# A macaron decoder layer on one core: first weights of output parts split ahead of the last gate, the memory's squares summed by token, the position table written by head, and row sums' tiles made in pairs

## The chip, the cores and the metric

The kernel runs on one core of a Trainium2 chip. The metric is the device time of one execution in microseconds (us), lower is better. A core has a matmul engine (PE, with its weight loads PEld), three engines for elementwise work (DVE, ACT, POOL), and SP, which here only issues DMAs. ACT and POOL issue DMAs too. Each engine works through its own instructions in order and waits for the others at semaphores.

## The reference

One layer on x (512 tokens by 1024), in float32, with a memory of 256 tokens. All but the mixer's scan and the softmaxes is matrix products:

```python
x = x + 0.5 * swiglu(rms_norm(x, w1), ffn1_w_in, ffn1_w_out)          # D_FF = 2816
x = x + hybrid_mixer(rms_norm(x, wm), ...)       # SSD heads + differential attention, out projection
x = x + memory_cross_attention(rms_norm(x, wc), rms_norm(mem, wmem), w_cq, w_ck, w_cv, w_co)
x = x + 0.5 * swiglu(rms_norm(x, w2), ffn2_w_in, ffn2_w_out)
return rms_norm(x, w_final)

def swiglu(h, w_in, w_out):
    gate, up = split(h @ w_in, 2)
    return (silu(gate) * up) @ w_out
```

`rms_norm(mem, w)` needs the sum of squares of each memory token over 1024 features. The differential attention adds a bias that depends on the distance of query and key only, one row of values for each of 8 heads.

## The kernel before, in words

**Numbers in two halves.** A float32 operand is split into a high part (fp32r, written by ACT, `split_into`, L155) and the rest (written by DVE, L156). A product is three matmuls: high by high, low by high, high by low. So every weight tile (512 KB, `wr`) that a DMA brings in becomes `wh` on ACT and then `wl` on DVE before PE can use it. There are six `wr` buffers; activations, gates, sums and the like share a pool of 128x512 slots (`s2`), handed out in turn.

**FFNs by blocks.** The two FFNs are computed with products of 2x2 blocks (Strassen's scheme). In the first FFN the inner width is taken in three thirds (`ffn1`, loop over `THIRDS`). In each, `ffn_quads` forms gate and up products (`qa`, `qb`, `qe`), multiplies them (`gated`: the gate's activation on ACT L442, the products on DVE L444), and `block_tiles` splits the result into the blocks 11, 22, 12 and the sums S1 to S4 (`g11h`, `s31h`, `s24h`, `gh` on ACT and their low parts on DVE). All but the last of these are spawned as chains with steps some us apart; the last is done at once.

Then `out_blocks` multiplies by the output weights of the third, in parts of two tiles: `product` over B11 into `oa`, over B12 + B11 (S1) into `oe`, in turn part by part, then S2 into `ob`, block 12 into `oa`, S3 into `ob`, S4 into `oe`, block 22 into `ob`. Sums of weight blocks are made on the way: `added` fetches one block by SP (L1220) and adds the other by an accumulating DMA that POOL issues (L1265); `t2` adds a third block on DVE (L1275). The fetches of the first two thirds are 512 KB; in the third third the second part has half the width.

**Order.** `Order` (`od`) interleaves one dense stream, which keeps a clock `od.t` of PE's work, with spawned chains that become due at times given in their `yield`s. That fixes the order in which the instructions are written down. SP and POOL keep this order; PE, ACT and DVE are ordered by a scheduler with its own estimates, within limits such as `behind`, which keeps an instruction after others.

**Beside the third third** `beside` spawns `prepare` and `memory_in`. `prepare` loads the bias table and one-hot rows, multiplies them (`prel`), copies the result with a scale on ACT (`hot`), writes it to memory (`rel_d`, two DMAs on ACT's queue) and then expands it with one DMA of 2.6 MB to `rel_z`, 128 copies for each of 8 heads; the attention later reads its bias from there (`ask_bias`). `memory_in` loads the transposed memory, squares each of its 8 tiles on ACT, adds them on DVE (`nacc`), splits the tiles into `hm`, and `finish` sums over partitions with matmuls into `nps`.

**Row sums.** `row_of` turns a column of 1/rms values into a row spread over partitions: for its high and low part it makes a diagonal tile (`ndiag`, L368) and multiplies it with ones (`nrow`), one after the other: diag, matmul, diag, matmul. The norms use DVE for it, the SSD groups POOL (after `yield W["gn"]`).

Of the kernel before, what the change touches and what calls it, by code (L numbers as in the profile page):

```python
# [11 lines left out]
F32 = mybir.dt.float32  # L12
# [5 lines left out]
P = 128  # L18
T = 512
# [16 lines left out]
LEAD = 4  # L36

W = {"h0": 3.4, "hs": 3.3, "hv": 2.08, "hp": 6.75}
W |= {"g0": 8.28, "gc": 0.75, "gx": 0.92, "gb": 2.59, "gs": 0.51, "gt": 2.0, "gd": 6.9, "gy": 0.38, "gq": 11.02, "gn": 6.52}
W |= {"c0": 4.97, "cs": 3.0, "ct": 4.82}  # L40

SPLIT, AHEAD = 5, 2
# [58 lines left out]
def body(tc, a, dbg=None):  # L101
# [255 lines left out]
        G.tensor_tensor(col, v, mhalf[:, :nb], ALU.pow)  # L357
        return col

    def row_of(col, nb, first, second):  # L360
        ch = tiny.tile([P, nb], R32, tag="ch", name=nm("ch"))
        V.tensor_copy(ch, col)
        cl = small("cl", nb)
        V.tensor_tensor(cl, col, ch.bitcast(F32), ALU.subtract)
        pr = aux("nrow", (P, nb * P))
        for j, (eng, c) in enumerate(((first, ch.bitcast(F32)), (second, cl))):
            diag = s2("ndiag", R32, (P, nb, P))
            eng.tensor_tensor(diag, ident[:, None, :].to_broadcast([P, nb, P]), c[:, :, None].to_broadcast([P, nb, P]), ALU.mult)  # L368
            with behind(list(newest_mm)):
                mm(pr, ones_r, diag.rearrange("p a b -> p (a b)"), j == 0, j == 1)  # L370
        return pr

    class Stat:
# [14 lines left out]
        def finish(self, apart=2.5):  # L388
# [4 lines left out]
            yield from self.from_sums(ps, apart)  # L393

        def from_sums(self, ps, apart=2.5):
            nb = self.n // P
            self.col = inv_rms_cols(ps, nb, 1.0 / D, EPS)
            yield apart
            pr = row_of(self.col, nb, V, V)
            self.row = s2("row", shape=(P, nb * P))  # L400
            S.activation(self.row, pr, AF.Copy)

# [2 lines left out]

    def normed(st, c, dst, sums):

        both = small("nboth", 4)
        V.tensor_tensor(both, sums[:, :4], sums[:, 4:], ALU.add)
        yield from st.from_sums(both)  # L410
        hf = {}
        for k in range(KT + 1):
            if k < KT:
                hf[k] = s2("hf")
                V.scalar_tensor_tensor(hf[k], x[k], par[:, c + k : c + k + 1], st.row, ALU.mult, ALU.mult)
            if k > 0:
                dst.append(split("hn", hf.pop(k - 1)))
                yield 1.6
# [9 lines left out]
        else:  # L428
            V.tensor_tensor(th[:, 0:2], halves(pu), halves(gate), ALU.mult)

    def ffn_quads(xs, wq, st, nq, made, places, sums=None, fresh=False):

        for q in range(nq):
            for out in quad(xs, next(wq), next(sums) if sums else None, fresh and q == 0):
                if out is None:
                    yield
            gs, us = out
            gate, th = s4("gate"), s4("th")
            for i in range(2):
                row = st.row[:, None, i * H : (i + 1) * H].to_broadcast([P, 2, H])  # L440
                V.tensor_tensor(gate[:, 2 * i : 2 * i + 2], halves(gs[i]), row, ALU.mult)
            S.activation(gate, gate, AF.Silu)  # L442
            for i in range(2):
                V.tensor_tensor(th[:, places[i]], halves(us[i]), gate[:, 2 * i : 2 * i + 2], ALU.mult)  # L444
            made(th)
            yield

    BY_BLOCK = slice(0, None, 3), slice(1, 3)

    def block_tiles(g, n):  # L450
# [12 lines left out]
        def made(th):  # L463
            g.append({})
            if len(g) < n:
                od.spawn(steps(th, g[-1], 2.9), 2.9)
            else:
                for _ in steps(th, g[-1], 0.0):
                    pass
        return made  # L470

    def ffn_first(h, wa):
# [9 lines left out]
    def ffn1(h, wa, at_out, each, done):  # L482
        xs = []
        wq, plain = iter(a["f1q"]), a["f1i"]

        def by_token():
            for k in range(KT):
# [3 lines left out]
        for ti, (_, nf) in enumerate(THIRDS):  # L491
            g = []
            nq = nf // 2
            made = block_tiles(g, nq)
            if ti == 0:
                th, f = s4("th"), 0
                for ps in ffn_first(h, wa):
# [3 lines left out]
                        gated(*ps, st1.row, th, f)  # L501
                        f += 1
                made(th)
                col4, ncol4 = small("col4", 4, bufs=1), small("ncol4", 4, bufs=1)
# [16 lines left out]
                h.clear()  # L521
                od.spawn(by_token(), 8.0)
                nq -= NPLAIN // 2
            yield from ffn_quads(xs, wq, st1, nq, made, BY_BLOCK)
            at_out(ti)
            yield from out_blocks(a[f"f1b{ti}"], None, g, col4, ncol4, each if ti == len(THIRDS) - 1 else None)
        done()
        banks = [acc, aux, acc, aux]
        yield from turn(1, banks)
# [13 lines left out]
    def beside(ti):  # L543
        if ti == 0:
            od.spawn(lambdas())
        elif ti == 2:
            od.spawn(prepare())
            od.spawn(memory_in(hm), 1.0)
# [15 lines left out]
        od.spawn(normed(st_mix, C_MIX, h, squares), 2.0)  # L564
        od.spawn(block_sums_in_dram(), 10.0)

    od.spawn(st1.finish(), 18.0)
    od.add(ffn1(h1, wa_s, beside, square, fin1))


# [24 lines left out]
    def prepare():  # L595
        rel_sb = small("rel_sb", 8, bufs=1)[:NUM_BUCKETS]
        nc.sync.dma_start(rel_sb, a["rel_bias"])
        hot = [s2("hot", shape=(NUM_BUCKETS, H)) for _ in range(2)]
        for i in range(2):
            nc.sync.dma_start(hot[i], a["hot"][:, i * H : (i + 1) * H])  # L600
        rel_far = small("rel_far", 64, bufs=1)[:8]
        V.memset(rel_far, MASKED)
        yield 9.0
        prel = aux("prel", (8, T))
        for i in range(2):
            mm(prel[:, i * H : (i + 1) * H], rel_sb, hot[i], True, True)
        for c in range(T, RW, 64):
            S.dma_start(rel_d[:, c : c + 64], rel_far)
        yield 1.5
        for i in range(2):  # L610
            S.activation(hot[i][:8], prel[:, i * H : (i + 1) * H], AF.Copy, scale=-8.0)
        yield 2.0
        for i in range(2):
            S.dma_start(rel_d[:, i * H : (i + 1) * H], hot[i][:8])
        yield 6.0
        S.dma_start(rel_z[:, :, :RW], rel_d[:, None, :].to_broadcast([8, P, RW]))

    def bc_c(t):
        return t[:, None, :].to_broadcast([P, 4, 16])
# [99 lines left out]
    def queries_keys(hd):  # L719
        if hd == 0:  # L720
            ask_bias(0)
        if hd < 7:
            ask_bias(hd + 1)
        pq = acc("pq")
        yield from proj(pq, load_w(a["wq"][hd]), h)
        q = split("q", pq, -1.0)
# [147 lines left out]
    def group(g, bt, ct, xs, zs):  # L874
# [99 lines left out]
        rh = small("rh", 4)  # L974
        V.tensor_scalar(rh, rr, 0.5, None, ALU.mult)
        yield W["gn"]
        pr = row_of(rh, 4, G, G)
# [10 lines left out]
    def memory_tile(k, queue=nc.sync):  # L988
        mk = s2("mem", shape=(P, MEM))
        queue.dma_start(mk, a["memT"][k])  # L990
        return mk

    def memory_in(dst):
        mem = []
        for k in range(0, KT, 2):
# [216 lines left out]
    def out_blocks(blocks, sums, g, col4, ncol4, each=None, finale=None, clean=True):  # L1212


        n = len(g)
        parts = [(k, min(k + 2, n)) for k in range(0, n, 2)]

        def fetch(of, part):
# [20 lines left out]
                    newest_mm[:] = [nc.tensor.matmul(ps, a_[:, ts], b_[:, ws], start=first and k == 0 and j == 0, stop=k == n - 1 and j == 2, skip_group_check=True).ins]  # L1239
                yield  # L1240

        def product(ps, of, which, first=False):
            for part in parts:
                w = weights(of, part)
                for t in range(2):
                    yield from some(ps[t], w, which, part, t, first)

# [3 lines left out]
            if each is not None and done:  # L1251
                each(tb, half_)

        bank = [acc, aux]
        a_ps = [bank[t]("oa") for t in range(2)]
        e_ps = [bank[t]("oe") for t in range(2)]
        b_ps = [bank[t]("ob") for t in range(2)]
        if clean:
            nc.tensor.matmul(b_ps[1], ones_r, ones_r[:, None, :].to_broadcast([P, 4, P]), start=True, stop=True)
        t_raw = {}  # L1260

        def added(of, more):
# [144 lines left out]
def layout(i):  # L1407
# [7 lines left out]
    d = {}  # L1415
    d["xT"] = np.ascontiguousarray(i["x"][0].T).reshape(KT, P, T)
    d["xt"] = np.ascontiguousarray(i["x"][0].reshape(4, P, 2, T).transpose(2, 0, 1, 3)).reshape(KT, P, T)
    d["memT"] = np.ascontiguousarray(i["mem"][0].T).reshape(KT, P, MEM)
    for n, s in (("1", "ffn1"), ("2", "ffn2")):
        wi = tiles(i[f"{s}_w_in"][0]).reshape(2 * NF, P, KT // 2, 2, P)  # L1420
# [58 lines left out]
```

## Time and profile before

| | us |
|---|---|
| median of 3 runs | 1327.48 |
| lowest and highest | 1323.78, 1330.71 |
| the profiled execution | 1326.33 |
| its span | 1324.2 |
| PE busy in it | 1295.8 |

Times in the rows of a profile are counted from the start of the span. Rows of a timeline give start, duration, engine, line, operation, output from inputs, and in brackets how long the engine stood idle before and what released it. A trailing h or l in a tile's name is the high or low part. Rows of windows give the stretch, its length, the busy time and instructions of PE, PEld, DVE, ACT and POOL, the granted clock of PE as a share, the DMA engines' share and GB/s.

### The profile page before, as it was taken

Reading aid. Unit: us, or ns where it says so; the run is one execution under the profiler, and the core shown is the slowest. Engines: PE = TensorE matmul, PEld = TensorE weight load, DVE = VectorE, ACT = ScalarE, POOL = GpSimd, SP = SyncE. Lnnn points to the kernel's source line nnn. Section 1 sums busy time; section 2 is a strip of 40 time slices with the busy share of each in tenths; the row PEclk is TensorE's granted clock in tenths of the full one; section 3 lists DMA queues with packets and bytes.
Section 4 is the critical chain, followed back from the end, with each engine's and each line's share of the span. In section 5 each row is a group of like instructions: output and inputs, shape, how many; then the busy total and the mean of one; then the engine's idle time right before and its main releaser. Section 6 shows DMA issues by size and latency. Waiting matters only on the chain.

```text
span 1324.2 us, 20141 instructions
## 1 busy us (share of the span) xinstructions
PE 1295.8 (98%) x7728; PEld 1127.3 (85%) x7728; DVE 988.1 (75%) x1570; ACT 708.4 (53%) x1192; POOL 124.8 (9%) x143
## 2 busy tenths in 40 slices
PE   9999999998989999999999999999999999999996
PEld 7898998897877778777788877888889999989995
DVE  7988789787866586557867686645678878877886
ACT  6544556455844465336644556434455645555564
POOL 0001010001110011110112021020001000000001
PEclk9999999999999999999999999999999999999998
DMA  7567767874794533763465547684238876656662
GB/s 272 163 171 211 179 176 198 216 204 122 241 351 133 154 66 97 252 176 100 92 201 180 167 128 232 196 208 142 65 96 244 227 226 185 189 193 178 186 203 87
DMA packets 69431, 235.28 MB, mean 178 GB/s; under 512 B 8072, under 2 KB 9576, under 8 KB 68984
## 3 DMA queue, kind: packets, MB, share of 16 engines
q1 hardware_dynamic: 52912, 180.19, 40.1%
q0 software_dynamic: 12880, 44.62, 19.0%
q10 hardware_dynamic: 3544, 9.20, 1.9%
q8 instruction: 60, 0.98, 0.3%
q14 instruction: 35, 0.29, 0.1%
HBM read 231.82 MB, written 50.91 MB: 214 GB/s over the span
## 4 chain that ended last, share of the span: by engine, by line
PE 86%; issue 7%; DVE 4%; DMA 1%; ACT 1%; POOL 1%; POOLq 0%; ACTq 0%; DVEq 0%
PE qb L240 12%; PE pm L146 9%; PE qe L240 8%; PE qa L240 8%; PE ob L1239 6%; PE pxbc L146 5%; PE oe L1239 4%; PE oa L1239 4%; PE pk L146 3%; PE pq L146 3%; PE pcq L146 3%; PE pv L146 3%; PE pz L146 2%; PE pa L146 2%; PE pg L146 2%
## 5 line engine op out<-in xcount | busy, mean ns | idle before, releaser
L155 ACT ACTIVATE wh<-wr 128x1024 fp32r<-128x1024 f32 (+1 forms) x329 | 334.6, 1019 | 368.8 <-issue 54.6
L156 DVE TENSOR_TENSOR wl<-wr,wh 128x1024 fp32r<-128x1024 f32 (+1 forms) x329 | 386.1, 1176 | 141.5 <-ACT wh L155 139.1
L146 PE MATMUL pxbc<-hnh,wh 128*128 128x512 f32 x128 | 52.3, 408 | 0.0
L146 PE MATMUL pxbc<-hnh,wl 128*128 128x512 f32 x128 | 50.3, 393 | 0.0
L146 PE MATMUL pxbc<-hnl,wh 128*128 128x512 f32 x128 | 50.2, 392 | 0.0
L748 ACT ACTIVATE ec<-ec,mn 128x512 f32<-128x512 f32 (+3 forms) x64 | 35.4, 555 | 24.1 <-DVE mn L747 24.1
L240 PE MATMUL qb<-s31h,wh 128*128 128x256 f32 x152 | 43.1, 284 | 0.0
L240 PE MATMUL qe<-s31h,wl 128*128 128x256 f32 x152 | 43.1, 283 | 0.0
L240 PE MATMUL qa<-h11h,wh 128*128 128x256 f32 x152 | 43.1, 283 | 0.0
L240 PE MATMUL qa<-h11h,wl 128*128 128x256 f32 x152 | 43.0, 283 | 0.0
L240 PE MATMUL qb<-s24h,wl 128*128 128x256 f32 x152 | 43.0, 283 | 0.0
L240 PE MATMUL qa<-hmh,wh 128*128 128x256 f32 x152 | 43.0, 283 | 0.0
L240 PE MATMUL qa<-hml,wh 128*128 128x256 f32 x152 | 43.0, 283 | 0.0
L240 PE MATMUL qe<-s24h,wh 128*128 128x256 f32 x152 | 43.0, 283 | 0.0
L240 PE MATMUL qe<-s24l,wh 128*128 128x256 f32 x152 | 43.0, 283 | 0.0
L240 PE MATMUL qe<-s24h,wl 128*128 128x256 f32 x152 | 43.0, 283 | 0.0
L240 PE MATMUL qb<-hmh,wh 128*128 128x256 f32 x152 | 43.0, 283 | 0.0
L240 PE MATMUL qb<-hml,wh 128*128 128x256 f32 x152 | 43.0, 283 | 0.0
L240 PE MATMUL qb<-hmh,wl 128*128 128x256 f32 x152 | 43.0, 283 | 0.0
L240 PE MATMUL qb<-s24l,wh 128*128 128x256 f32 x152 | 43.0, 283 | 0.0
L240 PE MATMUL qb<-s24h,wh 128*128 128x256 f32 x152 | 43.0, 283 | 0.0
L240 PE MATMUL qb<-s31h,wl 128*128 128x256 f32 x152 | 43.0, 283 | 0.0
(447 smaller groups left out, 4184.3 us busy)
## 6 DMA issues: line engine op xcount, KB each, us to landing
wr<-in_f2q SPq DMA_DIRECT2D x44, 512.0 KB, 4.4
wr<-in_f1q SPq DMA_DIRECT2D x40, 512.0 KB, 4.6
wr<-in_f1b SPq DMA_DIRECT2D x30, 512.0 KB, 4.9
isum<-in_f2q SPq DMA_DIRECT2D x22, 512.0 KB, 5.3
wr<-isum SPq DMA_DIRECT2D x22, 512.0 KB, 4.5
wsum<-in_f2b SPq DMA_DIRECT2D x20, 512.0 KB, 5.1
wr<-wsum SPq DMA_DIRECT2D x20, 512.0 KB, 4.6
wr<-in_f1q POOLq DMA_DIRECT2D x16, 512.0 KB, 6.4
```

The source lines that it names most:

```text
L146: newest_mm[:] = [nc.tensor.matmul(out, w, x, start=start, stop=stop).ins]
L155: S.activation(hi, src, AF.Copy),
L156: V.tensor_tensor(lo, src, hi.bitcast(F32), ALU.subtract),
L240: newest_mm[:] = [nc.tensor.matmul(out, a_[:, wc], b_, start=first and f == 0 and kp == 0 and j == 0, stop=kp == n - 1 and j == 2, skip_gr ...
L748: S.activation(ec[:, :n], ec[:, :n], AF.Exp, bias=mn, scale=-1.0, accum_out=sm[c][:, i : i + 1])
L1239: newest_mm[:] = [nc.tensor.matmul(ps, a_[:, ts], b_[:, ws], start=first and k == 0 and j == 0, stop=k == n - 1 and j == 2, skip_group_che ...
```

## The change

- `out_blocks` gets the number of its parts ahead of time and is begun inside `ffn_quads`, before the last gate of each third of the first FFN (`prime`): it fetches and splits the first part's weights of B11 and S1 there, and yields. The last `block_tiles` is placed behind these splits (`tied`).
- The memory's sums of squares come from a second layout of the memory (`memt`, by token): four tiles of 128x512, loaded on SP in the second third, squared on ACT with a sum along the row. The eight squares, the additions and the matmuls into `nps` go.
- `rel_z` is expanded by head: heads 0 and 1 by ACT's queue in `prepare`, the other six by SP's queue, one in the step of each of the heads 0 to 5.
- `row_of` makes both diagonal tiles, yields (`apart`), and does both matmuls. The planned times gq and gn change, gr is new.

```diff
+W |= {... "gq": 11.8, "gn": 5.0, "gr": 3.0}        # were gq 11.02, gn 6.52
-    def row_of(col, nb, first, second):
+    def row_of(col, nb, first, second, apart):
...
+        diags = []
+        for eng, c in ((first, ch.bitcast(F32)), (second, cl)):
+            diags.append(s2("ndiag", R32, (P, nb, P)))
+            eng.tensor_tensor(diags[-1], ident..., c..., ALU.mult)
+        yield apart
         pr = aux("nrow", (P, nb * P))
-        for j, (eng, c) in enumerate(((first, ch.bitcast(F32)), (second, cl))):
-            diag = s2("ndiag", R32, (P, nb, P))
-            eng.tensor_tensor(diag, ident..., c..., ALU.mult)
-            with behind(list(newest_mm)):
-                mm(pr, ones_r, diag..., j == 0, j == 1)
+        with behind(list(newest_mm)):
+            for j in range(2):
+                mm(pr, ones_r, diags[j]..., j == 0, j == 1)
...
     def ffn_quads(..., prime=None):
             gs, us = out
+            if prime and q == nq - 1:
+                next(prime)
             gate, th = s4("gate"), s4("th")
...
     def made(th):
-                for _ in steps(th, g[-1], 0.0):
-                    pass
+                with behind(list(recent) if tied else []):
+                    for _ in steps(th, g[-1], 0.0):
+                        pass
...
     def ffn1(h, wa, at_out, each, done):
+            out = out_blocks(a[f"f1b{ti}"], None, g, col4, ncol4, ..., n=nq)
-            yield from ffn_quads(xs, wq, st1, nq, made, BY_BLOCK)
+            yield from ffn_quads(xs, wq, st1, nq, made, BY_BLOCK, prime=out)
             at_out(ti)
-            yield from out_blocks(a[f"f1b{ti}"], None, g, col4, ncol4, ...)
+            yield from out
...
     def beside(ti):
+        elif ti == 1:
+            od.spawn(memory_squares())
...
     def prepare():
-        S.dma_start(rel_z[:, :, :RW], rel_d[:, None, :].to_broadcast([8, P, RW]))
+        for hd in range(2):
+            expand_bias(S, hd)
+
+    def expand_bias(queue, hd):
+        queue.dma_start(rel_z[hd, :, :RW], rel_d[hd : hd + 1].to_broadcast([P, RW]))
...
     def queries_keys(hd):
+        if hd < 6:
+            expand_bias(nc.sync, hd + 2)
...
+    def memory_squares():
+        mt = [s2("memt") for _ in range(4)]
+        for j in range(4):
+            nc.sync.dma_start(mt[j], a["memt"][j])
+        yield 12.0
+        for j in range(4):
+            with behind(list(recent)):
+                S.activation(mt[j], mt[j], AF.Square, accum_out=msq[:, j : j + 1])
+            yield 4.0
 
     def memory_in(dst):
...
-                st_mem.add(mk)
...
-        yield 3.0
-        yield from st_mem.finish(10.0)
+        both = small("nboth", 4, bufs=2)[:, :2]
+        V.tensor_tensor(both, msq[:, :2], msq[:, 2:], ALU.add)
+        yield from st_mem.from_sums(both, 10.0)
...
     def out_blocks(..., n=None):
+        ready = [None, None]
+        if early:
+            ready = [weights(of, parts[0]) for of in (blocks[B11], sums[0])]
+            yield
         bank = [acc, aux]
...
-        both = [product(a_ps, blocks[B11], "11", True), product(e_ps, sums[0], S1, True)]
+        both = [product(a_ps, blocks[B11], "11", True, ready[0]), product(e_ps, sums[0], S1, True, ready[1])]
```

The host lays the memory out a second time for `memt`.

More of the change, by code (lines that the diff above doesn't have):

```diff
@@ L38 @@
 W = {"h0": 3.4, "hs": 3.3, "hv": 2.08, "hp": 6.75}
-W |= {"g0": 8.28, "gc": 0.75, "gx": 0.92, "gb": 2.59, "gs": 0.51, "gt": 2.0, "gd": 6.9, "gy": 0.38, "gq": 11.02, "gn": 6.52}
+W |= {"g0": 8.28, "gc": 0.75, "gx": 0.92, "gb": 2.59, "gs": 0.51, "gt": 2.0, "gd": 6.9, "gy": 0.38, "gq": 11.8, "gn": 5.0, "gr": 3.0}
 W |= {"c0": 4.97, "cs": 3.0, "ct": 4.82}
@@ L364, in row_of @@
         V.tensor_tensor(cl, col, ch.bitcast(F32), ALU.subtract)
-        pr = aux("nrow", (P, nb * P))
-        for j, (eng, c) in enumerate(((first, ch.bitcast(F32)), (second, cl))):
-            diag = s2("ndiag", R32, (P, nb, P))
-            eng.tensor_tensor(diag, ident[:, None, :].to_broadcast([P, nb, P]), c[:, :, None].to_broadcast([P, nb, P]), ALU.mult)
-            with behind(list(newest_mm)):
-                mm(pr, ones_r, diag.rearrange("p a b -> p (a b)"), j == 0, j == 1)
+        diags = []
+        for eng, c in ((first, ch.bitcast(F32)), (second, cl)):
+            diags.append(s2("ndiag", R32, (P, nb, P)))
+            eng.tensor_tensor(diags[-1], ident[:, None, :].to_broadcast([P, nb, P]), c[:, :, None].to_broadcast([P, nb, P]), ALU.mult)
+        yield apart
+        pr = aux("nrow", (P, nb * P))
+        with behind(list(newest_mm)):
+            for j in range(2):
+                mm(pr, ones_r, diags[j].rearrange("p a b -> p (a b)"), j == 0, j == 1)
         return pr
@@ L386, in add, with finish @@
                 V.tensor_tensor(self.acc, self.acc, sq, ALU.add)
-        def finish(self, apart=2.5):
+        def finish(self, apart=2.5, rows=1.2):
             nb = self.n // P
@@ L392, in finish, with from_sums @@
                 mm(ps[:, b : b + 1], self.acc[:, b * P : (b + 1) * P], ones[:, 0:1], True, True)
-            yield from self.from_sums(ps, apart)
-        def from_sums(self, ps, apart=2.5):
+            yield from self.from_sums(ps, apart, rows)
+        def from_sums(self, ps, apart=2.5, rows=1.2):
             nb = self.n // P
@@ L398, in from_sums @@
             yield apart
-            pr = row_of(self.col, nb, V, V)
+            pr = yield from row_of(self.col, nb, V, V, rows)
             self.row = s2("row", shape=(P, nb * P))
@@ L406, in normed @@
     def normed(st, c, dst, sums):
-        both = small("nboth", 4)
+        both = small("nboth", 4, bufs=2)
         V.tensor_tensor(both, sums[:, :4], sums[:, 4:], ALU.add)
@@ L429, in gated, with ffn_quads @@
             V.tensor_tensor(th[:, 0:2], halves(pu), halves(gate), ALU.mult)
-    def ffn_quads(xs, wq, st, nq, made, places, sums=None, fresh=False):
+    def ffn_quads(xs, wq, st, nq, made, places, sums=None, fresh=False, prime=None):
         for q in range(nq):
@@ L448, in body, with block_tiles @@
     BY_BLOCK = slice(0, None, 3), slice(1, 3)
-    def block_tiles(g, n):
+    def block_tiles(g, n, tied=False):
         def steps(th, blocks, apart):
@@ L484, in ffn1 @@
         wq, plain = iter(a["f1q"]), a["f1i"]
+        col4, ncol4 = small("col4", 4, bufs=1), small("ncol4", 4, bufs=1)
         def by_token():
@@ L493, in ffn1 @@
             nq = nf // 2
-            made = block_tiles(g, nq)
+            made = block_tiles(g, nq, True)
+            out = out_blocks(a[f"f1b{ti}"], None, g, col4, ncol4, each if ti == len(THIRDS) - 1 else None, n=nq)
             if ti == 0:
@@ L503, in ffn1 @@
                 made(th)
-                col4, ncol4 = small("col4", 4, bufs=1), small("ncol4", 4, bufs=1)
                 V.tensor_scalar(col4, st1.col, 0.5, None, ALU.mult)
@@ L523, in ffn1 @@
                 nq -= NPLAIN // 2
-            yield from ffn_quads(xs, wq, st1, nq, made, BY_BLOCK)
+            yield from ffn_quads(xs, wq, st1, nq, made, BY_BLOCK, prime=out)
             at_out(ti)
-            yield from out_blocks(a[f"f1b{ti}"], None, g, col4, ncol4, each if ti == len(THIRDS) - 1 else None)
+            yield from out
         done()
@@ L565, in fin1 @@
         od.spawn(block_sums_in_dram(), 10.0)
-    od.spawn(st1.finish(), 18.0)
+    od.spawn(st1.finish(rows=0.0), 18.0)
     od.add(ffn1(h1, wa_s, beside, square, fin1))
@@ L976, in group @@
         yield W["gn"]
-        pr = row_of(rh, 4, G, G)
+        pr = yield from row_of(rh, 4, G, G, W["gr"])
         for j in range(2):
@@ L991, in memory_tile @@
         return mk
+    msq = small("msq", 4, bufs=1)
+    def memory_squares():
[7 more added lines that the diff above has]
+            yield 4.0
     def memory_in(dst):
@@ L1210, in block_sums_in_dram, with out_blocks @@
                 yield 9.0
-    def out_blocks(blocks, sums, g, col4, ncol4, each=None, finale=None, clean=True):
-        n = len(g)
+    def out_blocks(blocks, sums, g, col4, ncol4, each=None, finale=None, clean=True, n=None):
+        early = n is not None
+        n = n or len(g)
         parts = [(k, min(k + 2, n)) for k in range(0, n, 2)]
@@ L1240, in some, with product @@
                 yield
-        def product(ps, of, which, first=False):
+        def product(ps, of, which, first=False, ready=None):
             for part in parts:
-                w = weights(of, part)
+                w = ready if ready and part == parts[0] else weights(of, part)
                 for t in range(2):
@@ L1252, in update @@
                 each(tb, half_)
[L1254 to L1259, printed above, removed]
         t_raw = {}
@@ L1285, in out_blocks @@
             sums = [t1, added(blocks[B12], blocks[B22]), t2, lambda part: t_raw[part]]
-        both = [product(a_ps, blocks[B11], "11", True), product(e_ps, sums[0], S1, True)]
+        ready = [None, None]
+        if early:
+            ready = [weights(of, parts[0]) for of in (blocks[B11], sums[0])]
+            yield
+        bank = [acc, aux]
+        a_ps = [bank[t]("oa") for t in range(2)]
+        e_ps = [bank[t]("oe") for t in range(2)]
+        b_ps = [bank[t]("ob") for t in range(2)]
+        if clean:
+            nc.tensor.matmul(b_ps[1], ones_r, ones_r[:, None, :].to_broadcast([P, 4, P]), start=True, stop=True)
+        both = [product(a_ps, blocks[B11], "11", True, ready[0]), product(e_ps, sums[0], S1, True, ready[1])]
         for _ in parts:
@@ L1417, in layout @@
     d["xt"] = np.ascontiguousarray(i["x"][0].reshape(4, P, 2, T).transpose(2, 0, 1, 3)).reshape(KT, P, T)
+    d["memt"] = np.ascontiguousarray(i["mem"][0].reshape(2, P, 2, T).transpose(2, 0, 1, 3)).reshape(4, P, T)
     d["memT"] = np.ascontiguousarray(i["mem"][0].T).reshape(KT, P, MEM)
```

## The prediction

> **What bounds the kernel now.** I read the page first (busy time by engine, the chain that ended last), then the waits of PE, then the timelines of PE, ACT, DVE, POOL and SP around each of them.
>
> ```profile
> PE 1295.8 (98%) x7728; PEld 1127.3 (85%) x7728; DVE 988.1 (75%) x1570; ACT 708.4 (53%) x1192; POOL 124.8 (9%) x143
> PE 86%; issue 7%; DVE 4%; DMA 1%; ACT 1%; POOL 1%; POOLq 0%; ACTq 0%; DVEq 0%
> ```
>
> PE is busy 1295.8 of 1324.2 us. The change takes next to no matmul away, so it can only act on the 28 us that are left, on slow-clock matmuls behind long gaps, and on gaps that it makes itself. The waits of PE say where those 28 us are:
>
> ```profile
> PE oe L1239 <- ACT wh L155: 4.4, 1, 4.4
> PE pck L146 <- DVE wl L156: 3.8, 1, 3.8
> ...
> PE oe L1239 <- DVE wl L156: 1.7, 1, 1.7
> PE nrow L146 <- POOL ndiag L368: 1.1, 1, 1.1
> PE pm L146 <- DVE x L825: 0.9, 1, 0.9
> PE pn L146 <- POOL ysq L967: 0.8, 2, 0.5
> ...
> PE oe L1239 <- DVE s31l L156: 0.6, 1, 0.6
> PE nrow L146 <- DVE ndiag L368: 0.5, 1, 0.5
> ```
>
> The edits aim at four of these rows: the first weights of S1 (oe, 4.4), the cross-attention keys (pck, 3.8), and the two nrow rows. A long gap costs more than its length:
>
> ```profile
> 319.73 0.80 PE L1239 MATMUL oe<-wh,s31h 128*128 128x512 f32 x1 [4.44 <-ACT wh L155]
> 324.34 0.39 PE L1239 MATMUL oa<-wh,g11h 128*128 128x512 f32 x1
> 319.70:323.20 3.50, 3.43 (x8) 2.29 (x9) 3.49 (x5) 1.02 (x2) 0.00 (x0) 0.52 0.13 28
> 375.00:378.00 3.00, 3.00 (x17) 3.00 (x17) 3.00 (x5) 1.40 (x3) 0.00 (x0) 0.55 0.99 329
> ```
>
> Behind the 4.44 us gap the granted clock (third number from the end) is 0.52 for 3.5 us. The twelve oe matmuls take 324.34 - 319.73 = 4.61 us; at the usual spacing (below) they would take 2.73, so the slow clock costs 1.9 us. Behind the 3.8 us gap the clock is 0.55 for 3 us: 3 x 0.45 = 1.4 us.
>
> **Second third of the first FFN: the memory loads.** Here the change adds four loads of memt, put on SP's queue behind the two primed fetches and ahead of the second parts of B11 and B12. They take generic 128x512 slots. By the built order the fourth load may start only when the last gate product (th<-c,gate) has read its slot, and all later SP fetches stand behind it.
>
> ```profile
> 199.63 32.47 SPq L1220 DMA_DIRECT2D wr<-in_f1b  x10
> 212.70 0.40 PE L1239 MATMUL oa<-wh,g11h 128*128 128x512 f32 x1
> 215.82 0.68 DVE L444 TENSOR_TENSOR th<-c,gate 128x512 f32<-128x512 f32 x1
> 216.10 1.06 ACT L155 ACTIVATE wh<-wr 128x1024 fp32r<-128x1024 f32 x1 [0.92 <-DMA wr<-in_f1b]
> 217.19 1.22 DVE L156 TENSOR_TENSOR wl<-wr,wh 128x1024 fp32r<-128x1024 f32 x1 [0.70 <-ACT wh L155]
> 218.16 0.39 PE L1239 MATMUL oa<-wh,g11h 128*128 128x512 f32 x1
> 220.88 0.39 PE L1239 MATMUL oe<-wh,s31h 128*128 128x512 f32 x1
> wr<-in_f1b SPq DMA_DIRECT2D x7, 512.0 KB, 4.9
> DMA to landing us min/median/max: 6.1/7.2/8.3
> ```
>
> In these rows SP issues the out-weights from 199.63 on, long before they are needed. PE does B11 and S1 of the first part from 212.70 (24 matmuls to 218.16, 0.2275 each), B11 of the second part at 218.16 and S1 of the second part at 220.88. The last row is POOL's accumulating DMA (L1265) in 216 to 240 us, the next to last SP's fetch around here.
>
> After the change: gate product ends about 216.4 (215.82 + 0.68, perhaps a little less as DVE is freer); fourth memt issued about 216.4; B11 second part about 216.8, landed 4.9 later, 221.7; its wh 222.8 (1.06). PE wanted it at 218.16: a wait of 4.6, then wl 1.22 behind wh against two matmuls of 0.23, another 0.8, then the slow clock. But the end is set by B12: issued about 217.2, landed 222.1, accumulated on POOL 7.2, 229.3, wh 230.4. S1 of the second part starts at 230.4 in place of 220.88, 9.5 later; the first wait lies inside this. The 0.6 on s31l, which stood there, goes (with its ramp 0.7); wl (0.3) and some slow clock (0.5) come on top. **Loss 9.6.** Upper bound: the accumulate at 8.3 and the full slow clock, 9.6 + 1.1 + 1.4, with 0.6 for wl behind other DVE work: 12.7. Lower bound: SP doesn't hold, and only ACT's new order counts, in which wh of B11's second part stands behind gate, g11h, s31h, s24h and gh. From the third third:
>
> ```profile
> 312.38 0.40 PE L1239 MATMUL oa<-wh,g11h 128*128 128x512 f32 x1
> 318.12 0.61 ACT L155 ACTIVATE gh<-th 128x512 fp32r<-128x512 f32 x1
> ```
>
> gh ends 6.35 after the first oa, so here at 219.05; wh at 220.1, 2.0 late, and 0.8 for wl: loss 2.7. I take 9.6, since the slot and the queue order are both fixed in the built program and only durations are open.
>
> [...]
>
> **Third third: priming.** S1's first wh now stands ahead of the gate, so the 4.4 us wait and its 1.9 us go: oa and oe of the first part run 312.38 to 317.83.
>
> ```profile
> 329.20 1.02 PE L146 MATMUL prel<-hot,rel_sb 32*8 32x256 f32 x4
> 330.26 0.64 ACT L611 ACTIVATE hot<-prel 8x256 f32<-8x256 f32 x2 [1.33 <-PE prel L146]
> 330.66 0.63 ACTq L614 DMA_DIRECT2D rel_d<-hot  x2
> 335.08 0.74 ACTq L616 DMA_DIRECT2D rel_z<-rel_d  x1
> wr<-in_f1b SPq DMA_DIRECT2D x1, 256.0 KB, 2.6
> 327.59 1.74 POOL L1265 DMA_DIRECT2D wr<-in_f1b  x2 [19.87 <-DVE x L1250]
> wr<-in_f1b POOLq DMA_DIRECT2D x2, 512.0 KB, 5.6
> 336.40 0.39 PE L1239 MATMUL ob<-wh,s31h 128*128 128x512 f32 x1
> 342.91 0.50 PE L1239 MATMUL oe<-wl,s24h 128*128 128x512 f32 x1 [1.73 <-DVE wl L156]
> ```
>
> But the built order now puts prel right behind that oe (to 318.85), and on ACT hot, both rel_d issues and two rel_z issues, which wait for rel_d to land, ahead of wh of B11's second part. From these rows: hot from 318.9, rel_d issued by 319.9. The landing of rel_d has no row; between 0 and the 2.6 of a 256 KB load, I take 2.3, since the two DMAs are tiny and most of it is not bytes: 322.2. Then two rel_z issues (under 0.74 each, say 0.8 together) and wh (0.62 at half width, by gh's row): 323.6. PE waits 4.8 in place of 4.4, slow clock again. B11's second part then runs to 326.9, S1's to 328.2; before, S1's second part ran from 325.70 (4.44 + 1.9 behind) to 327.06, and prel (1.0), then still due, is already done: 0.2 late. B12's accumulate for S3 is issued once the sum behind the late wl is done (325.5), landed 330.3, accumulated (5.6) 335.9, wh 337.0, against 336.6 when PE wants it: 0.4. The 1.73 us wait for wl at 342.91 can shrink, as the memory's squares and their additions are gone from ACT and DVE: I take 1.0 of it. **Gain 0.4**; from 4 lost (accumulate at 8.3 and the 1.73 staying) to 3 gained (rel_d landing at once).
>
> **Table by head.**
>
> ```profile
> SPq L174 <- DMA rel_z<-rel_d: 14.5, 1, 14.5
> 369.23 1.06 ACT L155 ACTIVATE wh<-wr 128x1024 fp32r<-128x1024 f32 x1 [6.40 <-DMA wr<-in_wck]
> 374.65 0.58 PE L146 MATMUL pck<-hm,wl 128*128 128x256 f32 x1 [3.80 <-DVE wl L156]
> ```
>
> SP stands 14.5 us until the 2.6 MB rel_z has landed; the keys' weights come late, ACT waits 6.4 and PE 3.8. With two heads on ACT's queue and six singly on SP's, nothing in the built order waits for so long a transfer. What goes is 3.8 and 1.4 of slow clock. The same bytes still move beside the weights (DMA share 0.99 in 375 to 378), so I leave 0.4: **gain 4.8**, between 0 and 5.2.
>
> **Row sums in pairs.** Both ndiag tiles are made, then a yield of 1.2 (3.0 for groups), then both matmuls. That lifts the nrow waits, 1.1 and 0.5; gn falls from 6.52 to 5.0 and gq rises to 11.8, which can move pn's 0.8 and pm's 0.9 either way. **Gain 1.6**, from 1 lost (pn a tile late) to 2.5. The squares by token replace eight Squares, seven additions and two nps matmuls by four Squares and an addition; on PE that is nothing, its cover being that ACT is 53% busy.
>
> **The sum.** 9.6 - 0.4 - 4.8 - 1.6 = 2.8 us lost. Against the profiled execution's 1326.33 (span 1324.2 and 2.1 around it): 1329.1. The median of the runs shown is 1.15 higher: 1330.3, 0.2% slower. About 0.5% (6.6 us) is what a measurement of this kernel can tell from no change, so my number lies inside that.
>
> **Rivals.**
> (a) Everything dearer: POOL's accumulate at its slow end in both thirds, 12.7 and 4 lost: 1330.3 + 3.1 + 4.4 = 1337.8. For it: five queued 512 KB fetches then share the DMA engines with it. Against: 7.2 already holds some of that.
> (b) The loads don't hold SP, because the fourth slot's last reader is an earlier product than I read, and only ACT's order costs: 2.7 for 9.6, 1323.4; with rel_d landing at once, 1320.8: faster than before. It decides if B12's second part is issued before about 207.7 (220.88 less 1.06, 7.2 and 4.9). For it: SP ran 13 us ahead before (199.63 against 212.70). Against: the gate product needs the last qb, which ends at 212.7.
> (c) The pck wait stays, because the six table DMAs on SP or the DMA share replace it: 1335.1. Against: they are placed behind the keys' weights.
>
> **Chances.** Forecast 0.40, of which 0.07 ends slower by over 0.5% and 0.33 within it; (a) 0.25, slower; (b) 0.25, 0.15 faster by over 0.5% and 0.10 within; (c) 0.10, slower. Faster 0.15, same 0.43, slower 0.42. The range 1319 to 1341 takes in (b) with most of its bonus and (a) with 3 us on top.
>
> **What would show it.** Right: in the profile after, a PE wait of some 4 us on oa's wh and another ahead of oe in the second third, with SP's second-part fetches issued after 216 us; no S1 wait of 4.4 in the third third but one of 4 to 5 on oa behind rel_z's issue; no 14.5 us wait of SP on rel_z and no pck wait over 1; no nrow wait over 0.5. Wrong: second-part fetches issued before 210, PE's gap in the third third under 2, or new waits in the head stage behind the six table DMAs.

## The result: slower, 1341.14 us against 1328.5, and the profile after

The changed kernel takes 1341.14 us (median of 4 runs, 1339.67 to 1341.93); the kernel before takes 1328.5 (1323.78 to 1330.71, now in four runs). The ratio is 1.0099, interval 1.0069 to 1.0128. That is slower by about 1%, beyond the forecast of 1330.3 and just outside its range (up to 1341). The profiled execution has a span of 1339.8 us, 15.6 more than before. That is 3 us more than the medians differ by (12.6), so what the traces say of the size of a stage holds for one execution of each kernel.

The waits of PE after the change, in the same form as before (waiting engine, tile, line, what it waited for, total, times, longest):

```profile
PE oa L1266 <- ACT wh L155: 7.9, 3, 4.0
PE oe L1266 <- ACT wh L155: 7.7, 2, 5.5
PE pq L146 <- DVE vl L156: 3.7, 1, 3.7
...
PE ob L1266 <- ACT wh L155: 0.9, 1, 0.9
PE pn L146 <- POOL ysq L982: 0.8, 1, 0.8
```

The pck wait of 3.8 and both nrow waits are gone, as meant. In their place stand waits for split weights (oa, oe) of 15.6 us in all and a new one of 3.7 on values (pq for vl). Where they stand is seen by setting the same product's start in the two traces side by side:

| product | before | after | later by | change since the row above |
|---|---|---|---|---|
| second third, first oa | 212.70 | 213.16 | 0.5 | |
| third third, first oa | 312.38 | 326.58 | 14.2 | +13.7 |
| transposes pxf, behind the first FFN | 350.75 | 369.90 | 19.2 | +5.0 |
| first pq, behind the keys | 384.46 | 397.38 | 12.9 | -6.2 |
| pk behind the values and pq | 578.10 | 596.49 | 18.4 | +5.5 |
| first qe of the second FFN | 1000.70 | 1016.46 | 15.8 | -2.6 |

**Second third (+13.7).** Timelines of SP, DVE, ACT, POOL and PE of the changed kernel:

```profile
204.93 11.90 SPq L1013 DMA_DIRECT2D memt<-in_memt  x4
216.88 19.72 SPq L1247 DMA_DIRECT2D wr<-in_f1b  x8
215.79 0.68 DVE L449 TENSOR_TENSOR th<-c,gate 128x512 f32<-128x512 f32 x1
221.26 1.06 ACT L155 ACTIVATE wh<-wr 128x1024 fp32r<-128x1024 f32 x1 [1.74 <-DMA wr<-in_f1b]
223.80 0.85 POOL L1286 DMA_DIRECT2D wr<-in_f1b  x1 [23.72 <-DVE wl L156]
232.67 1.06 ACT L155 ACTIVATE wh<-wr 128x1024 fp32r<-128x1024 f32 x1 [6.35 <-DMA wr<-in_f1b]
222.37 0.80 PE L1266 MATMUL oa<-wh,g11h 128*128 128x512 f32 x1 [3.34 <-ACT wh L155]
233.78 0.79 PE L1266 MATMUL oe<-wh,s31h 128*128 128x512 f32 x1 [5.52 <-ACT wh L155]
238.91 0.40 PE L1266 MATMUL ob<-wh,s24h 128*128 128x512 f32 x1
```

SP spends 11.9 us on the four memory loads; the last is issued when th<-c,gate has ended (215.79 + 0.68), and the output weights follow from 216.88, where before they were issued from 199.63. B11's second part is split at 221.26, B12's second part is accumulated by POOL from 223.80 and split at 232.67. PE waits 3.34 and 5.52, and both times restarts slowly (matmuls of 0.63 us and a spacing of 0.43 in place of 0.2275). Three rows give the sizes: SP's output-weight fetches in 213 to 232, POOL's accumulate there, and the window of the first restart and the second wait:

```profile
wr<-in_f1b SPq DMA_DIRECT2D x7, 512.0 KB, 7.6
wr<-in_f1b POOLq DMA_DIRECT2D x1, 512.0 KB, 8.8
222.00:232.00 10.00, 5.86 (x12) 3.64 (x12) 2.45 (x2) 0.90 (x2) 0.85 (x1) 0.67 0.96 301
```

The 7.6 is a median. The fetch of B11's second part landed faster: it was issued at 216.88 and its split began at 221.26. In the kernel before, POOL's accumulate of the same tile stood here, with its time to landing:

```profile
206.87 0.85 POOL L1265 DMA_DIRECT2D wr<-in_f1b  x1 [9.95 <-DVE wl L156]
DMA to landing us min/median/max: 9.1/9.1/9.1
```

So this accumulate was no slower after the change (8.8 for 9.1); it only began 16.9 us later.

**Third third (+5.0, with the old wait of 4.4 gone).** Timelines of ACT and PE, and the waits of SP:

```profile
333.21 0.64 ACT L620 ACTIVATE hot<-prel 8x256 f32<-8x256 f32 x2 [0.26 <-PE prel L146]
333.61 0.63 ACTq L623 DMA_DIRECT2D rel_d<-hot  x2
335.27 1.22 ACTq L629 DMA_DIRECT2D rel_z<-rel_d  x2
336.53 0.63 ACT L155 ACTIVATE wh<-wr 128x512 fp32r<-128x512 f32 x1 [2.68 <-issue]
337.21 0.50 PE L1266 MATMUL oa<-wh,g11h 128*128 128x512 f32 x1 [4.04 <-ACT wh L155]
355.69 0.79 PE L1266 MATMUL oe<-wh,s24h 128*128 128x512 f32 x1 [2.17 <-ACT wh L155]
SPq L1247 <- DMA rel_d<-hot: 17.2, 1, 17.2
```

ACT issues rel_z ahead of the split of B11's second part, as forecast, and PE waits 4.04. The last row was not forecast: SP stands 17.2 us, until rel_d has landed, ahead of a fetch of output weights that has nothing to do with it. In the built program that fetch is given the same completion semaphore (the counter that tells of a DMA's landing) as the second rel_d DMA, eight DMAs earlier in the written order, and may start only when that one has landed. All later output weights come late, and PE pays again at S3 (0.9) and S4 (the wait of 2.17).

**Keys (-6.2).** PE's waits have no row for pck any more. SP's one wait for rel_z is 1.5 us in place of 14.5.

**Values (+5.5).** PE, ACT and DVE of the changed kernel, then PE and ACT of the kernel before at the same place:

```profile
583.63 0.62 PE L146 MATMUL nrow<-ndiag,ones_r 128*128 128x512 f32 x2
584.28 1.41 DVE L995 SCALAR_TENSOR_TENSOR y<-y,par,nrow 128x512 f32<-128x512 f32 x2 [2.22 <-PE nrow L146]
585.07 0.63 ACT L155 ACTIVATE ysh<-y 128x512 fp32r<-128x512 f32 x1 [4.26 <-DVE y L995]
587.20 2.04 ACT L155 ACTIVATE vh<-pv 128x512 fp32r<-128x512 f32 x4
589.30 0.50 PE L146 MATMUL pq<-hnh,wh 128*128 128x512 f32 x1 [3.66 <-DVE vl L156]
```

```profile
567.32 0.62 PE L146 MATMUL nrow<-ndiag,ones_r 128*128 128x512 f32 x2
571.05 1.55 ACT L155 ACTIVATE vh<-pv 128x512 fp32r<-128x512 f32 x3
572.58 0.45 PE L146 MATMUL pq<-hnh,wh 128*128 128x512 f32 x1
```

Before, the row of sums came 5.3 us ahead of pq; after, seven matmuls ahead of the end of the values. ACT holds the splits of y ahead of those of the values in its order; they wait for nrow, the values' splits stand behind them, and pq needs the bank that these free. The wait of 3.66 and the slow restart behind it (24 pq matmuls in 7.19 us for 5.52) take 5.3 us.

### The profile page after: what moved, and what is told of

The parts are those of the page before. It is cut to its first block, busy times and chain, and to the rows that moved or that the text cites. A ratio compares the mean times of both kernels' runs of the same rounds, so it can differ in the third digit from the quotient of the medians.

```text
span 1339.8 us, 20126 instructions
## 1 busy us (share of the span) xinstructions
PE 1303.0 (97%) x7724; PEld 1131.8 (84%) x7724; DVE 985.9 (74%) x1564; ACT 709.6 (53%) x1192; POOL 124.0 (9%) x143
## 3 DMA queue, kind: packets, MB, share of 16 engines
q0 software_dynamic: 12880, 44.62, 19.2%
## 4 chain that ended last, share of the span: by engine, by line
PE 91%; DMA 3%; DVE 3%; ACT 2%; issue 1%; POOL 0%; ACTq 0%; SPq 0%; POOLq 0%; DVEq 0%
PE qb L240 12%; PE pm L146 9%; PE qe L240 8%; PE qa L240 8%; PE pxbc L146 7%; PE ob L1266 6%; PE oe L1266 4%; PE oa L1266 4%; PE pq L146 3%; PE pk L146 3%; PE pcq L146 3%; PE pz L146 3%; PE pv L146 3%; PE pck L146 2%; PE pcv L146 2%; PE pg L146 2%
## 5 line engine op out<-in xcount | busy, mean ns | idle before, releaser
L240 PE MATMUL qa<-hmh,wl 128*128 128x256 f32 x152 | 43.0, 283 | 0.0
L240 PE MATMUL qa<-h11l,wh 128*128 128x256 f32 x152 | 43.0, 283 | 0.0
```

The costliest lines, as they stand in the source:

```text
L240: newest_mm[:] = [nc.tensor.matmul(out, a_[:, wc], b_, start=first and f == 0 and kp == 0 and j == 0, stop=kp == n - 1 and j == 2, skip_gr ...
```

## The experiments

Each was timed against the kernel before on the same chip; so the ratios are compared, with the changed kernel's 1.0099 as the mark (0.001 is 1.3 us). The theory after the result: three separate losses, in SP's queue at the memory loads, in SP's queue and ACT's order at rel_d, and in the place of the row of sums.

**1. Memory loads later in SP's queue (mem_late).**

```diff
-            od.spawn(memory_squares())
+            od.spawn(memory_squares(), 14.0)
```

> The changed kernel (1341.1 us) with one edit: the chain with the four memory loads starts 14 us later, so that they are written on SP's queue behind the second parts of B11, B12 and B22 and not ahead of them. Theory Q (SP stands at the fourth load's slot, and all fetches behind it come late): the whole loss of the second third, 14.4 us, goes down to 1 or less, 1341.1 - 13.5 = 1327.5, within 2. Rival A (ACT's new order, gate and its tiles ahead of the second part's wh): 2.7 of it stays, 1330. Rival M (the loads' bytes and the squares themselves slow the third): 5 or more stays, 1333 or above.

Measured: 1333.42 us, ratio 1.0041 (1.0028 to 1.0054). About 7.6 us came, half of what theory Q said, and rival M's number was met. SP's timeline speaks for another place of the same wait:

```profile
209.33 9.68 SPq L1013 DMA_DIRECT2D memt<-in_memt  x4
219.11 19.54 SPq L1247 DMA_DIRECT2D wr<-in_f1b  x6
```

The loads now stand ahead of block 21 and the rest, and still need a slot that the last gate's products free; the next weights are issued at 219.11. So SP stood at a slot again, one place later. In the trace the second third loses 7.5 us in place of 13.7.

**2. Memory loads behind all output weights (mem_end).** The same edit with 34.0.

> The changed kernel (1341.1 us) with the memory loads' chain started 34 us later: all four loads are written behind the last output weights of the second third, where their slots have long been read. Theory Q (any place ahead of output weights makes SP stand at a slot): the remaining loss of the 14 us version (1333.4) goes too, 1326 to 1329. Rival M (that version's rest is the loads' traffic and the squares): 1333.

Measured: 1327.85, ratio 1.0015 (1.0000 to 1.0031). The same four loads with the same bytes and squares:

```profile
200.48 32.27 SPq L1247 DMA_DIRECT2D wr<-in_f1b  x10
232.80 1.85 SPq L1013 DMA_DIRECT2D memt<-in_memt  x4
223.60 0.50 PE L1266 MATMUL oe<-wh,s31l 128*128 128x512 f32 x1 [0.34 <-DVE s31l L156]
```

SP is back at 200.48, the loads take 1.85 us to issue in place of 11.9, and PE's waits for output weights in this third are gone; 0.34 on s31l is left. Against the changed kernel that is 0.0084, 11 us. Theory Q holds and rival M falls: bytes and squares are the same. In the trace the second third is 0.6 us longer than before the change. Rival A is not told apart by this run alone, since with its fetches written early ACT's order has the second part's split ahead of the gate again, as before; but experiment 1 has that order too and still lost 7 to 8 us, so SP's standing is the larger cause by far.

**3. prel held (prel_late).** The two matmuls are put behind the matmuls written before them; prel, hot, rel_d and rel_z follow later.

```diff
+        with behind(list(newest_mm)):
             for i in range(2):
                 mm(prel[:, i * H : (i + 1) * H], rel_sb, hot[i], True, True)
```

> The changed kernel with one edit: the two prel matmuls are held behind the matmuls written before them, so that prel, hot, rel_d and rel_z come after the second parts' first products, as before the change. Theory L (in the third third SP stood 17.2 us until rel_d had landed and ACT waited for it ahead of a wh): both waits go and the third third is 8 to 12 us shorter, 1329 to 1333. Rival P (POOL's accumulating DMAs and the weights' transfers are the limit there): 4 us shorter at most, 1337 or above.

Measured: 1334.48, ratio 1.0055 (1.0035 to 1.0076): 5.8 us by ratio, between the two theories' numbers. The stage by itself speaks for theory L: from its first oa to the transposes pxf the third third takes 43.3 us in the changed kernel's trace, 35.1 here and 38.4 before, 8.2 less than changed. The whole time shows less, in part because other stages differ between traced executions: the second third, which this edit leaves alone, lost 15.9 us here against 13.7. PE's waits in the third third fall to this:

```profile
338.11 0.50 PE L1267 MATMUL oa<-wh,g11h 128*128 128x512 f32 x1 [1.29 <-ACT wh L155]
354.75 0.50 PE L1267 MATMUL ob<-wl,s31h 128*128 128x512 f32 x1 [1.07 <-DVE wl L156]
```

**4. Only rel_z held (rel_z_held).** rel_z goes behind later weight splits; prel and rel_d stay early.

```diff
+        with behind(list(recent)):
             for hd in range(2):
                 expand_bias(S, hd)
```

> The changed kernel with the two rel_z issues on ACT held behind later weight splits; prel and rel_d stay early, and one fetch of SP (half of B22) still waits for rel_d to land before it may use its semaphore. Theory L1 (ACT's wait for rel_d ahead of the wh of B11's second part is the loss): as good as holding prel, 1334 to 1335. Theory L2 (SP's wait for rel_d, 17.2 us, is the loss): SP still issues late, and at most 2 us come, 1339 or above.

Measured: 1338.15, ratio 1.0083 (1.0059 to 1.0107): 2 us by ratio, inside what the intervals leave open, so the verdict is read from the rows:

```profile
SPq L1248 <- DMA rel_d<-hot: 16.8, 1, 16.8
332.73 0.50 PE L1267 MATMUL oa<-wh,g11h 128*128 128x512 f32 x1 [1.79 <-ACT wh L155]
350.90 0.50 PE L1267 MATMUL ob<-wl,s31h 128*128 128x512 f32 x1 [3.23 <-DVE wl L156]
```

ACT's part is away (4.04 to 1.79), SP's wait of 16.8 stays and PE pays 3.23 at S3, where with prel held it pays 1.07. The third third takes 39.7 us, by the measure of experiment 3: about 3.7 of the 8.2 come with ACT's part, and about 4.6 only when prel is held too and SP's wait goes with it. Both paths were losses; L2, SP's, is somewhat the larger.

**5. The planned times of before (rows_timing_old).** Both diagonal tiles are still made ahead of both matmuls.

```diff
-"gq": 11.8, "gn": 5.0, "gr": 3.0
+"gq": 11.02, "gn": 6.52, "gr": 0.0
```

> The changed kernel with the planned times as before the change (gq 11.02, gn 6.52, gr 0), the two diagonal tiles still made ahead of both matmuls. Theory G (the later row of sums pushes the copies of y ahead of the value splits on ACT, and PE waits 3.7 us for vl with 1.5 us of slow clock behind it): 4 to 5 us less, 1337. Rival H (the wait comes from the table's DMAs in the head stage): no difference, 1341.

Measured: 1337.71, ratio 1.0072 (1.0051 to 1.0093): 3.6 us. The waits of PE have no vl row left, and these rows are back:

```profile
PE nrow L146 <- POOL ndiag L368: 1.1, 1, 1.1
PE pn L146 <- POOL ysq L982: 0.8, 2, 0.5
```

That fits theory G. From the first pq behind the keys to pk behind the values this trace keeps its distance from the kernel before (13.8 us at both), where the changed kernel loses 5.5. Behind that, the changed kernel gains 1.8 up to the start of the second FFN and this one nothing: 5.5 less 1.8 is the 3.7 that the new times cost. Rival H falls, since the table's DMAs were untouched.

**6. All three edits (all_three).** Experiments 1, 3 and 5 together.

> The changed kernel with the three edits together (memory loads later, prel held, planned times as before). If the three losses stand in different stages and add up: 1341.1 - 13.5 - 10 - 4 = 1313.5, below the kernel before (1328.5). Rival S (a stage that is freed starts its transfers earlier and runs into the next limit): half of the last two comes, 1320 or above.

Measured: 1323.44, ratio 0.9966 (0.9952 to 0.9980). The three gains add up: 0.0058 + 0.0044 + 0.0027 is 0.0129, and 1.0099 less that is 0.9970. The expected 1313.5 was missed by 9.9: singly, the first edit had already fallen short by some 6 us and prel_late by 4.

**7. The same with the loads at the end (all_three_end).** Experiment 2 in place of 1.

> The changed kernel with memory loads at the end of the second third, prel held, and planned times as before. Theory: the 1323.4 of the three edits with the 14 us delay, less the 5 to 6 us that its second third still lost: 1317 to 1319. Rival S: the later loads collide with the gate weights of the third third, 1323.

Measured: 1316.51, ratio 0.9927 (0.9907 to 0.9947), faster than both kernels.

**8. The kernel before with the table by head alone (before_by_head).**

> The kernel before (1328.0 in these runs) with only the table written by head, two heads on ACT's queue and six on SP's. Theory: SP no longer stands 14.5 us at rel_z, the pck wait of 3.8 and its slow clock of 1.4 go: 5 less, 1323, and 7 less if the weights of the first q come earlier too, as between the profiles before and after (20.0 to 12.9 late). Rival C (the six later transfers cost as much among the heads' weights): no difference, 1328.

Measured: 1322.02, ratio 0.9970 (0.9956 to 0.9984), 4 us. In the traces the transposes ahead of the keys stand within 0.1 us of the kernel before (the third third's start within 0.4), and the first pq stands 5.6 us earlier (378.87 for 384.46). PE's wait at pck is 0.2 in place of 3.8. The time shows 4 of these 5.6. Rival C falls.

**9. The best without priming (best_no_priming).** out_blocks begins after the last gate again, but still fetches and splits both first weights before anything else of it.

```diff
-            yield from ffn_quads(xs, wq, st1, nq, made, BY_BLOCK, prime=out)
+            yield from ffn_quads(xs, wq, st1, nq, made, BY_BLOCK)
```

> The kernel with all three edits and the loads at the end (0.9927 of the kernel before), without priming: the first weights are fetched and split after the last gate again. Theory: the 4.4 us wait on S1's first weights and its 1.9 us of slow clock come back, less the 2 to 3 us that priming costs at the second part's first weights: 3 to 5 us slower than with it, 0.996. Rival: priming only moves the wait, as in the changed kernel: no difference, 0.993.

Measured: 1316.52, ratio 0.9927 (0.9902 to 0.9952): no difference. The wait of 4.4 does not come back. ACT of this kernel in the third third:

```profile
310.62 1.06 ACT L155 ACTIVATE wh<-wr 128x1024 fp32r<-128x1024 f32 x1 [1.77 <-PE qe L240]
314.35 1.06 ACT L447 ACTIVATE gate<-gate 128x1024 f32<-128x1024 f32 x1 [2.67 <-DVE gate L446]
```

S1's split still runs ahead of the gate. Two differences to the kernel before can hold it there: both first weights are written at once at the start of out_blocks, and the last block's splits stay behind the weights' (`tied`). Which of them does it was not tried, nor whether the other edits (the squares gone from this third, prel held) have a share.

**10. The best with the row of sums in between (best_rows_apart).** gq 10.2, gn 5.0, gr 2.3.

> The same best kernel with the planned times gq 10.2, gn 5.0, gr 2.3: the row of sums stands 19 matmuls ahead of the end of the values (7 in the changed kernel, 22 before), and in the last groups where the changed kernel has it. Theory G (only the place in the value stage was wrong): nrow's 1.1 us wait and half of pn's go and no wait for vl comes, 2 to 3 us less, 0.991. Rival: the ACT copies of y still come ahead of the values' splits and PE waits for vl, 1 to 2 us more, 0.994.

Measured: 1314.70, ratio 0.9909 (0.9886 to 0.9932). The median is 1.8 us below that of all_three_end; the intervals overlap, so a gain is not shown. In the profile nrow stands at 560.42 and pq at 565.00 with no wait ahead of it, and the 1.1 us wait on nrow is gone.

**11. The best with the old squares (best_old_squares).** The eight squares and seven additions of before, no memt.

> The same best kernel with the memory's squares as before the change (eight squares and seven additions in the third third, no memt). Theory: ACT and DVE have room, and the squares by token bring little: no difference within 2 us, 0.993. Rival: the additions and squares make the wl wait in the third third (1.7 before) come back: 2 to 3 us more, 0.995.

Measured: 1317.58, ratio 0.9936 (0.9912 to 0.9961): 1 us more, within the intervals. A wl wait at S4 is back (1.07), as the rival said, at half of its price; but the kernel of experiment 9, with the new squares, has one of 1.07 there too, so it is not shown to come from the squares. What the squares by token bring once their loads are out of the way is too small to tell here; where the change put the loads, they cost eleven.

## Why the prediction was wrong

It forecast a loss of 2.8 us as the sum of terms of both signs; the medians give 12.6 and the traces 15.6. Nearly all the signs that it named for being right were seen (the waits on oa and oe, SP's fetches after 216, no S1 wait of 4.4, no pck wait, no nrow wait); two losses stood where it named no sign. Term by term, by the traces:

- **Second third: right mechanism, mis-sized.** 9.6 was forecast, 13.7 measured. The steps up to the fetch were right within half a microsecond: gate product done 216.4 (216.47), fetches from 216.8 (216.88), B11's second part landed 221.7 (221.2). The failed sizes are those on B12's way and the restart. POOL's wait for B12's own fetch ended at 223.3 and its accumulate began at 223.80, not at 222.1: that fetch, one of five let go within 2.1 us, took 5.9 in place of 4.9, and POOL's start came on top. (The bracket of POOL's row names DVE's wl, but that ended at 223.58, behind POOL's wait.) The accumulate took 8.8 and not 7.2: the 7.2 is the middle of two later accumulates (those in 216 to 240), while this one had taken 9.1 in the trace before, above even the 8.3 of the upper bound. So B12's second part was split at 232.67 and not at 229.3. And the slow clock, which came behind both waits, counts behind the second: 12 oe matmuls took 238.91 - 233.78 = 5.1 us, not 2.7, where 0.5 was allowed. The upper bound of 12.7 was nearly enough. mem_end shows that the cause is the place in SP's queue.
- **The Trainium skill's two figures.** The Trainium skill's page "DMA: Bandwidth & Descriptors", section "Anatomy of one DMA — SWDGE (gpsimd) path", gives 2.0 us and the bytes at 436 GB/s for a DMA that GpSimd issues. By that an estimate for POOL's 512 KB is 3.2 us; the section does not speak of accumulating, and the accumulate took 8.8 beside queued fetches at a DMA share of 0.96. It has no price for SP's fetches, which took 4.3 to 8.2 here. The Trainium skill's page "TensorE: Matmul & The Clock Gate", section "Part 1: The HAM clock gate", puts the fall of the clock behind an idle window of about 3.4 us. That fits the long waits (3.34, 4.04, 5.52 and 3.66 us). But behind the wait of 2.17 at 355.69 the matmuls are 0.43 apart, and the granted clock is 0.50 from 355.5 to 359:

```profile
355.50:359.00 3.50, 3.31 (x8) 2.64 (x9) 3.50 (x6) 1.76 (x6) 0.00 (x0) 0.50 0.32 109
```

  The measurement decides: one single idle time of 3.4 us is not needed. Another wait, of 0.89 at 352.29, lies 3 us ahead of it, but in mem_end a wait of 2.14 with only one of 0.31 some 3 us ahead of it was followed by a clock of 0.52 over 3.5 us. Nor do the lengths alone settle it: waits of 1.40 and 0.85 us, 2 us apart, in the second third were followed by a clock of 0.60 over 4 us in mem_late and of 1.00 in all_three. Before the change the 1.73 us at 342.91 had no such restart. What decides between these cases stays open.
- **Third third: the step that failed is "what is queued on SP".** 0.4 gained was forecast, 5.0 lost measured. ACT's path was right (PE's wait 4.04 for a forecast 4.8; wh started 9.95 us behind the third's first oa, forecast 10.6; rel_z was issued 1.0 us behind the end of the rel_d issues, where 2.3 was taken for the landing). Missing was SP: prel's earlier place also moved rel_d in the written order relative to SP's fetches, and one of them shares rel_d's completion semaphore. rel_z_held leaves that wait alone in place and PE still pays for it: about 4.6 of the 8.2 us that prel_late brings in this third. The same kind of wait, SP on rel_z, is quoted in the prediction as the reason for the keys' gap; for rel_d the prediction has no such step.
- **Table by head: right.** 4.8 forecast, 6.2 in these traces; alone on the kernel before 5.6 in the traces and 4 by time (2.1 to 5.8).
- **Row sums: wrong sign.** 1.6 gained was forecast; 5.5 lost at the values and 2.6 gained later, 2.9 lost. Of the 2.6, 0.8 stays with the old times (rows_timing_old), so it goes with the tiles made in pairs. The nrow waits went as said. The failed step is the bound "1 lost": it looked at pn and pm, not at what is queued behind the row of sums on ACT. The planned time moved the row to seven matmuls from the end of the values, and the splits of y then hold those of the values.
- **Priming: costed as the removal of 4.4 + 1.9 us.** The wait went, but best_no_priming loses it without priming as well.
- **Rivals.** (a), all dearer, was the nearest, and half of that is luck: in the second third POOL's accumulate was slow, as it says, but its 4 us for the third third came near the measured 5.0 by another way, SP's wait for rel_d. (b) fell: the slot's reader was the gate product. (c) fell.

## What to carry to other kernels

Here a load put early into an in-order DMA queue cost nothing that could be measured by its bytes (all_three_end with it, best_old_squares without), and 11 us by its destination. Before such a load is placed, find what must free its buffer, and when, and what is queued behind it. The same goes for completion semaphores that several queues share in turn: a tiny DMA on ACT's queue kept SP standing 17.2 us ahead of weights, which cost this third about 4.6 us, so a moved step's DMAs are to be checked against every later fetch, not only its readers. When a size is taken from a trace, take it from the very transfer that the chain goes through: the accumulate in question had 9.1 us there, and its neighbours' 7.2 went into the sum. And a row of sums that came later was not paid where it is computed but by what stood behind its consumer on the engine that splits the results.

## What the runs showed that was not expected

The change held gains that its losses hid: with the loads behind the output weights, prel held and the row of sums between its old and new place, the same edits give 0.9909 of the kernel before, where the change as it stood gave 1.0099. Fetches of 512 KB land in 4.9 us at the median when SP runs ahead and in 7.6 when held fetches are let go together. A PE wait of 2.17 us with one of 0.89 shortly before it was enough for a restart at half the clock, and a restart cost some 1.5 to 3 us beside its wait (1.7 behind the 3.66 at pq; the 12 oa matmuls from 222.37 took 5.7 us, not 2.7).
